# Block 3 of a three-block layer: where the filling of the last state chain and of the attention is emitted, and the order of two small products

## The chip, the core and the metric

The kernel runs on one core of a Trainium2 chip. TensorE (PE) multiplies matrices into PSUM, VectorE (DVE) and ScalarE (ACT) read PSUM and do the elementwise work, GpSimd (POOL) does elementwise work in SBUF, and SP, ACT and POOL issue DMAs. Each engine takes its instructions in one fixed order, and semaphores order the engines among each other. The metric is the device time of one execution in microseconds (us). The median of the three runs before is 3429.2 us (3425.64 to 3435.23).

## What is computed

Three transformer-like blocks run after each other on 512 tokens of width 1024. The change lies in the middle of the third, where a state recurrence (RWKV-7) and a sparse attention (NSA) run side by side and are joined by one output projection:

```python
for l in range(DEPTH):
    h = rmsnorm_3(x, norm1_g[l])
    proj = h @ w_in[l]
    ...
    k_cmp = rmsnorm_3(compress(kv_heads(kc), cmp_pos[l, 0], ...), k_norm_g[l, 0])
    ...
    o_nsa = nsa_attention(q, k_cmp, v_cmp, k_sel, kv_heads(vsl), k_win, kv_heads(vwn), gates, rel_bias)
    ...
    o_rwkv = rwkv7_time_mix(rw, ...)
    x = x + jnp.concatenate([o_nsa, o_rwkv], axis=-1) @ w_out[l]
    # then a convolved feed-forward block

def _wkv7_step(state, inp):
    r, w, k, v, a, b = inp
    sa = jnp.einsum('bhvk,bhk->bhv', state, a)
    state = state * w[:, :, None, :] + sa[..., None] * b[:, :, None, :] + v[..., None] * k[:, :, None, :]
    return state, jnp.einsum('bhvk,bhk->bhv', state, r)
```

## The kernel before

All activations lie features by tokens: a tile is 128 features by 512 tokens. A projection (`K.block`, lines L250 to L252) is 24 matmuls 128x128 by 128x512: eight chunks of the contraction, and three products for each, because both operands are split in a high and a low half (`zh`, `zl`, `wh`, `wl`). Its weights come by one DMA on SP (L239) and are split by ACT (L240) and DVE (L244). Products of the normed input show as `mm<-zh` or `mm<-zl`, those of the output projection as `mm<-nh` or `mm<-nl`. There are two PSUM buffers for such products in this part, two for small products (`s`), two for transposes (`t`) and two for accumulations (`o`).

**The recurrence** (`rwkv`) does two heads at a time, so four head pairs t = 0 to 3, and cuts the 512 tokens in 8 chunks of 64. For each pair `features` makes the operands, `prepare` solves the inside of the chunks, and `steps` walks the 8 chunks, each of which needs the state that the one before it leaves. That is the state chain. One step c is, in the program's order: `rr` (L1809, weight tile 128x64), an ACT copy to `rsb` (L1811), the product that closes the output of the step before (`own`, L1831, weight tiles 64x64), `y` (L1816, 128x64), `sa` (L1819, 64x64), two DVE copies (L1824), the state's product `ds` (L1834, 128x64), a DVE add and a DVE multiply (L1835, L1837). The last gives the next step its state. `finish` then norms the pair's output with two products with a constant (L1630, L483) and gates it (L1853).

**The filling.** A step of the chain leaves TensorE mostly waiting, so other work is emitted between its steps by pulling on Python generators. For t = 0 to 2 that is the preparation of the next pairs. For t = 3 it is `Nsa.prepare`, which makes the attention's keys and values: two weight loads of the compression (L1391, one buffer of 1 MB on SP), its sums on DVE into the one buffer `blk` (L1401), 32 products (L1406), a small chain behind them (L1420, L1426, L1439), and then twice the norm of a key (L483, L488, L489, three DVE operations L460 to L462, L1454, four ACT copies L305 and L307, two DVE operations L306) and the transposes of a value (L1462). Key and value share the one buffer `x3`, into which DVE writes each projection (L1901).

**The attention** (`Nsa.attend`) goes through 16 units: 4 pairs of heads, 2 heads, 2 branches. A unit makes its scores (L1535, L1536), a softmax on DVE, ACT and POOL (L1537, L1543, L1547), transposes (L1555), splits them (L282, L287) and multiplies with the values (L1560, L1561). Before every second unit a generator `prep` projects and norms the next queries (ending at L1492) and makes their compressed scores (L1503). Its filling (`fill`) is the half of the output projection that needs only the recurrence: 8 tiles, each of 12 products `mm<-nh`.

A scheduler fixes the order on each engine from this program text. What is emitted earlier has the right of way, and the slots of a pool with several buffers are given out in the order of emission: a tile emitted later waits for those emitted before it.

```python
for c, _ in enumerate(steps(yo, now)):
    if c < 6 or t == 3:
        next(nxt, None)
    next(more, None)
for _ in more:
    pass
finish(t, yo, bo)
```

Of the kernel before, what the change touches and what calls it, by code (L numbers as in the profile page):

```python
# [1353 lines left out]
class Nsa:  # L1354
# [113 lines left out]
    def attend(self, out, fill):  # L1468

        K, D, proj = self.K, self.D, self.proj  # L1470
        nc, tp = K.nc, K.tp
# [78 lines left out]
        def values(br, g, pt, o, last):  # L1550
            for jj in range(4):
                t = K.st()
                N = 512 - 128 * jj
                for i in range(jj, 4):
                    nc.tensor.transpose(t[:, 128 * (i - jj):128 * (i - jj) + 128],  # L1555
                                        pt[i][:, 128 * (i - jj):128 * (i - jj) + 128], K.ident)
                ph, pl = T("ph", dt=F32R, bufs=3)[:, :N], T("pl", dt=F32R, bufs=3)[:, :N]
                K.split(ph, pl, t[:, :N])
                w = vd[br, g][:, 3 - jj].rearrange("p e d -> p (e d)")
                nc.tensor.matmul(o[:, 512 - N:], w, ph, start=False, stop=False)  # L1560
                nc.tensor.matmul(o[:, 512 - N:], w, pl, start=False, stop=last and jj == 3)  # L1561
# [8 lines left out]
        for k, (j, s, br) in enumerate(units):  # L1570
            if (s, br) == (0, 0):
                nxt = prep(j + 1, ops[j + 1]) if j < 3 else iter(())
            next(nxt, None)
            if (s, br) == (1, 1):
                for _ in nxt:
                    pass
            now = pt
            if k < 15:
                pt = run(*units[k + 1])
            if br == 0:  # L1580
                o = K.so()
                w = vcd[j // 2][s].rearrange("p e d -> p (e d)")
                nc.tensor.matmul(o, w, ops[j][3], start=True, stop=False)
            values(br, j // 2, now, o, br == 1)
            if br == 1:
                K.unstack(out[j][64 * s:64 * s + 64], o)
            if k % 2:
                next(fill, None)
        for _ in fill:
            pass  # L1590
        self.pools.close()
# [2 lines left out]
def rwkv(K, D, proj, out, after):  # L1594

    tc, nc, tp = K.tc, K.nc, K.tp
    V = D["vec"]
    front = ExitStack()
    with K.tc.tile_pool(name="rwb", bufs=1, reuse_waits="tile", side="right") as rp:
# [199 lines left out]
        def steps(yo, sets):  # L1799

            nc.vector.memset(sets[0][3][:64, :, 0], 0.0)
            late = []
            for c in range(8):
                u, n = c // 4, c % 4
                lrb, xt, ml, vs, bk, wend = sets[u]
                w = K.so()
                rr, sa, ds = w[:, :64], w[:, 64:128], w[:64, 128:256]
                for s in range(2):
                    nc.tensor.matmul(rr[64 * s:64 * s + 64], ml[:, s, n, :64], vs[:, s, n], start=True, stop=True)  # L1809
                rs_ = TB("rsb", (P, 64), bufs=2)  # L1810
                nc.scalar.activation(rs_, rr, AF.Copy)  # L1811
                if late:
                    late.pop()()
                y = yo[:, c]
                for s in range(2):
                    nc.tensor.matmul(y[64 * s:64 * s + 64], vs[:, s, n], ml[:, s, n, 64:], start=True, stop=False)  # L1816
                for s in range(2):
                    h = slice(64 * s, 64 * s + 64)
                    nc.tensor.matmul(sa[h], xt[h, n], rs_[h], start=True, stop=True)  # L1819
                if c < 7:  # L1820
                    s0 = TB("s0", (64, 2, 64), bufs=2)
                    nc.vector.tensor_copy(s0, vs[:64, :, n])
                for s in range(2):
                    nc.vector.tensor_copy(vs[:64, s, n], sa[64 * s:64 * s + 64])  # L1824
                ss = TB("ssb", (P, 64), bufs=2)
                nc.scalar.activation(ss[64:], vs[:64, 1, n], AF.Copy)

                def own(y=y, ss=ss, lrb=lrb, vs=vs, n=n):
                    for s, x in enumerate((vs[:64, 0, n], ss[64:])):
                        h = slice(64 * s, 64 * s + 64)  # L1830
                        nc.tensor.matmul(y[h], x, lrb[h, n], start=False, stop=True)  # L1831
                if c < 7:
                    for s in range(2):
                        nc.tensor.matmul(ds[:, 64 * s:64 * s + 64], bk[:, s, n], vs[:, s, n], start=True, stop=True)  # L1834
                    nc.vector.tensor_add(s0, ds.rearrange("p (s d) -> p s d", s=2), s0)  # L1835
                    to = vs[:64, :, n + 1] if n < 3 else sets[1][3][:64, :, 0]
                    nc.vector.tensor_mul(to, s0, wend[:, :, n:n + 1].to_broadcast([64, 2, 64]))  # L1837
                late.append(own)
                if c == 7:
                    late.pop()()  # L1840
                yield

        def finish(t, yo, bo):

            y = K.tp.tile([P, 512], F32, name="tb")
            nc.scalar.activation(y, yo.rearrange("p n l -> p (n l)"), AF.Copy)
            s_ = mean64(y)
            nc.vector.tensor_sub(y, y, s_)
            rg = K.head_rstd(y, R0, 64e-5, rp)
            nc.vector.scalar_tensor_tensor(y, y, V("ln_x_w", t), rg, op0=ALU.mult, op1=ALU.mult)  # L1850
            nc.vector.scalar_tensor_tensor(y, y, V("ln_x_b", t), bo, op0=ALU.add, op1=ALU.add)
            s_ = K.ss()
            nc.tensor.matmul(s_, g2[:, 128 * t:128 * t + 128], xg, start=True, stop=True)  # L1853
            nc.vector.tensor_mul(y, s_, y)
            K.split(*out[t], y)
# [15 lines left out]
        for t in range(4):  # L1871
            bo, now, sets = fs[t][5], sets, []
            more = iter(())
            if t < 3:
                nxt = prepare(t + 1, *fs[t + 1], sets)
                if t < 2:
                    more = fg[t + 2]
            else:
                front.close()
                nxt = after()  # L1880
            yo = K.so([P, 8, 64])
            for c, _ in enumerate(steps(yo, now)):
                if c < 6 or t == 3:
                    next(nxt, None)
                next(more, None)
            for _ in more:
                pass
            finish(t, yo, bo)
# [15 lines left out]
def block3(K, D, hs, store):  # L1904
# [20 lines left out]
    o2 = [[op.tile([P, 512], F32R, name=f"n{e}{n}") for e in "hl"] for n in range(4, 8)]  # L1925
    att = Nsa(K, D, proj)
    rwkv(K, D, proj, o2, att.prepare)
    op = work.enter_context(tc.tile_pool(name="mx3a", bufs=1, reuse_waits="tile", side="right"))
    o1 = [op.tile([P, 512], F32, name=f"o{n}") for n in range(4)]
# [85 lines left out]
```

## Time and profile before

| | |
|---|---|
| median of three runs | 3429.2 us |
| the profiled execution | 3428.05 us |
| its span, first to last instruction | 3426.2 us |
| TensorE busy | 3309.6 us, 97% |
| mean granted TensorE clock | 0.988 of full speed |
| last state chain, first `rr` to last `own` | 2825.7 to 2879.5 us of the span |
| attention, first L1503 to last L1561 | 2902.6 to 3029.5 us |

Times inside the span are counted from its start. "Busy" TensorE means that some matmul is in flight, not that the array is full. A timeline row gives start, duration, engine, line, result and operands; several instructions of a line that follow each other are merged in a row, and an fp32 product shows as two passes, so two products are x4. A duration in brackets is idle time before the row, with what ended it.

### The profile page before, as it was taken

To read this page: it belongs to the slowest core of one execution; us is meant where nothing else is said; L and a number is where in the kernel's file an instruction comes from. 1 tells how busy PE (TensorE), PEld (TensorE's weight loads), DVE (VectorE), ACT (ScalarE), POOL (GpSimd) and SP (SyncE) were. 2 spreads that over 40 slices of the span, in tenths; PEclk is the share of its full clock that TensorE was granted. 3 is DMA by queue.
4 is the path that set the end of the run, shared out by engine and by line. 5 is a ranking of instruction groups with operands and counts; after the bars stand their busy time and mean duration, and the time that the engine had idled before them with its cause. 6 is when DMAs were issued, how large, how long until landed. Compare 5 with 4: busy or idle time off the path is not lost. (4 is left out here: it accounts for less than half of the span.)

```text
span 3426.2 us, 48101 instructions
## 1 busy us (share of the span) xinstructions
PE 3309.6 (97%) x19089; PEld 2717.3 (79%) x19089; DVE 1932.8 (56%) x3242; ACT 1404.0 (41%) x2474; POOL 712.4 (21%) x748
## 2 busy tenths in 40 slices
PE   8999999999999999999999999999999998999999
PEld 8999977778877888876777778788876766778887
DVE  4433366655754433268777564566446656766642
ACT  3222366653433322235555233444333434754431
POOL 2110133332122111112121231111113222421100
PEclk9999999999999999999999999999999999999999
DMA  3223222232223232323332322223331012122332
GB/s 120 90 93 88 86 85 78 69 97 95 66 86 102 92 99 90 96 94 85 106 100 86 111 81 98 92 93 98 104 115 34 31 46 87 41 64 96 98 101 91
DMA packets 89601, 298.61 MB, mean 87 GB/s; under 512 B 10711, under 2 KB 11351, under 8 KB 89120
## 3 DMA queue, kind: packets, MB, share of 16 engines
q1 hardware_dynamic: 76896, 260.70, 23.7%
q0 software_dynamic: 6416, 23.80, 2.4%
q10 hardware_dynamic: 6064, 11.03, 1.0%
q8 instruction: 150, 2.46, 0.3%
q14 instruction: 75, 0.61, 0.1%
HBM read 288.02 MB, written 7.47 MB: 86 GB/s over the span
## 5 line engine op out<-in xcount | busy, mean ns | idle before, releaser
L250 PE MATMUL mm<-zh,wh 128*128 128x512 f32 (+1 forms) x3296 | 1189.8, 361 | 20.2 <-ACT zh L291 8.4
L252 PE MATMUL mm<-zh,wl 128*128 128x512 f32 (+1 forms) x3296 | 1189.0, 361 | 3.8 <-DVE wl L244 3.7
L251 PE MATMUL mm<-zl,wh 128*128 128x512 f32 (+1 forms) x3296 | 1180.2, 358 | 3.1 <-DVE zl L292 3.1
L240 ACT ACTIVATE wh<-w 128x1024 fp32r<-128x1024 f32 (+2 forms) x523 | 523.8, 1001 | 1086.6 <-PE mm L251 759.0
L244 DVE TENSOR_TENSOR wl<-w,wh 128x1024 fp32r<-128x1024 f32 (+2 forms) x523 | 627.6, 1201 | 400.1 <-ACT wh L240 392.3
L250 PEld LDWEIGHTS mm<-zh,wh 128*128 128x128 f32 x3296 | 622.8, 189 | 115.6 <-issue 10.6
L251 PEld LDWEIGHTS mm<-zl,wh 128*128 128x128 f32 x3296 | 623.6, 189 | 100.6 <-DVE zl L292 4.1
L252 PEld LDWEIGHTS mm<-zh,wl 128*128 128x128 f32 x3296 | 622.6, 189 | 100.2 <-DVE wl L244 6.9
L250 PE MATMUL mm<-hh,wh 128*128 128x512 f32 (+1 forms) x880 | 308.5, 351 | 0.0
L251 PE MATMUL mm<-hl,wh 128*128 128x512 f32 (+1 forms) x880 | 308.3, 350 | 0.0
L252 PE MATMUL mm<-hh,wl 128*128 128x512 f32 (+1 forms) x880 | 307.6, 350 | 0.0
L251 PEld LDWEIGHTS mm<-hl,wh 128*128 128x128 f32 x880 | 165.6, 188 | 23.3
L250 PEld LDWEIGHTS mm<-hh,wh 128*128 128x128 f32 x880 | 165.5, 188 | 23.3
L252 PEld LDWEIGHTS mm<-hh,wl 128*128 128x128 f32 x880 | 165.6, 188 | 23.1
L382 POOL TENSOR_TENSOR ta<-ta,rs 128x264 f32<-128x264 f32 (+1 forms) x66 | 86.0, 1316 | 395.8 <-ACT ta L381 395.8
L334 POOL TENSOR_TENSOR acc<-acc,ta 128x512 f32<-128x512 f32 (+1 forms) x49 | 85.2, 1739 | 345.7 <-ACT ta L333 345.3
L1000 POOL TENSOR_TENSOR cv<-cv 128x512 f32<-128x512 f32 x44 | 57.6, 1309 | 434.0 <-DVE cv L981 397.6
L981 DVE SCALAR_TENSOR_TENSOR cv<-ta,vec,cv 128x510 f32<-128x510 f32 (+1 forms) x176 | 132.0, 753 | 3.2 <-ACT cv L978 0.3
L384 DVE TENSOR_TENSOR tb<-mm,ta 128x264 f32<-128x264 f32 (+1 forms) x66 | 32.8, 519 | 141.5 <-PE mm L252 137.7
L380 DVE TENSOR_TENSOR ta<-mm,rs 128x264 f32<-128x264 f32 (+1 forms) x66 | 32.5, 518 | 108.3 <-PE mm L252 108.3
L995 DVE TENSOR_TENSOR ta<-mm,rs 128x512 f32<-128x512 f32 x88 | 60.3, 687 | 57.9 <-PE mm L252 57.8
L282 ACT ACTIVATE hh<-cv 128x512 fp32r<-128x512 f32 x44 | 27.8, 632 | 144.7 <-POOL cv L1000 144.7
(592 smaller groups left out, 4645.3 us busy)
## 6 DMA issues: line engine op xcount, KB each, us to landing
w<-in_w_up_dram SPq DMA_DIRECT2D x176, 512.0 KB, 3.5
w<-in_w_in_dram SPq DMA_DIRECT2D x160, 512.0 KB, 3.5
w<-in_w_dn_dram SPq DMA_DIRECT2D x64, 512.0 KB, 3.5
w<-in_w_dn_dram SPq DMA_DIRECT2D x32, 384.0 KB, 3.1
w<-in_w_out_dram SPq DMA_DIRECT2D x16, 512.0 KB, 3.5
aB<-acum_d POOLq DMA_DIRECT2D x16, 512.0 KB, 5.9
w<-in_w_pb_dram SPq DMA_DIRECT2D x32, 256.0 KB, 2.9
negc<-negc_d POOLq DMA_DIRECT2D x8, 528.0 KB, 4.1
```

Of the source, the lines that this page charges most:

```text
L240: nc.scalar.activation(h_, w_, AF.Copy)
L244: nc.vector.tensor_sub(l_, w_, h_.bitcast(F32))
L250: nc.tensor.matmul(ps, wh, xh, start=start, stop=False)
L251: nc.tensor.matmul(ps, wh, xl, start=False, stop=False)
L252: nc.tensor.matmul(ps, wl, xh, start=False, stop=stop)
L334: nc.gpsimd.tensor_tensor(acc, acc, q, op=ALU.add)
L380: nc.vector.tensor_mul(ta, a, rs[:, c])
L382: nc.gpsimd.tensor_tensor(ta, ta, rs[:, c], op=ALU.mult)
L384: nc.vector.tensor_mul(tb, b, ta)
L981: nc.vector.scalar_tensor_tensor(y[:, d:], x[:, :T - d], w(i), y[:, d:], op0=ALU.mult, op1=ALU.add)
L995: nc.vector.tensor_mul(x, p, rs)
L1000: nc.gpsimd.tensor_tensor(y[1], y[1], y[0], op=ALU.mult)
```

## The change

Three edits. The attention no longer pulls on `fill` after every second unit, so that all of the filling is emitted behind the whole attention. In a step of the chain `sa` is emitted ahead of `y`. And the chain of t = 3 no longer pulls on `nxt`, so that `Nsa.prepare` is emitted behind the whole chain and its `finish`.

```diff
@@ Nsa.attend
             if br == 1:
                 K.unstack(out[j][64 * s:64 * s + 64], o)
-            if k % 2:
-                next(fill, None)
         for _ in fill:
             pass
@@ rwkv, steps
                 if late:
                     late.pop()()
+                for s in range(2):
+                    h = slice(64 * s, 64 * s + 64)
+                    nc.tensor.matmul(sa[h], xt[h, n], rs_[h], start=True, stop=True)
                 y = yo[:, c]
                 for s in range(2):
                     nc.tensor.matmul(y[64 * s:64 * s + 64], vs[:, s, n], ml[:, s, n, 64:], start=True, stop=False)
-                for s in range(2):
-                    h = slice(64 * s, 64 * s + 64)
-                    nc.tensor.matmul(sa[h], xt[h, n], rs_[h], start=True, stop=True)
@@ rwkv, the loop over the pairs
             for c, _ in enumerate(steps(yo, now)):
-                if c < 6 or t == 3:
+                if c < 6 and t < 3:
                     next(nxt, None)
```

No instruction is added or removed; what moves is their order. Lines behind the first edit are two lower in the changed kernel, and `sa` and `y` change places: `rr` is L1807, `sa` L1814, `y` L1817, `own` L1829, `ds` L1832, and in `finish` L1630 is L1628 and L1853 is L1851.

On TensorE, from the end of step 2 to the end of step 3 of the last chain, before:

```order
L1406 MATMUL s<-blk,w_24636 128x62 x16
L1809 MATMUL o<-h_24015,ml 64x64 x2
L1831 MATMUL o<-lrb,ssb 64x64
L1816 MATMUL o<-ml,h_24015 64x64 x2
L1420 MATMUL s<-h_24634,w_24527 64x62
L1819 MATMUL o<-rsb,xt 64x64 x2
L1831 MATMUL o<-lrb,h_24015 64x64
L1426 MATMUL s<-sq,cst 64x62
L1834 MATMUL o<-h_24015,h_24016 64x64 x2
L1439 MATMUL s<-w_24527,h_24731 31x64 x2
L1831 MATMUL o<-lrb,ssb 64x64
L483 MATMUL s<-hsq,cst 128x512
```

The same place in the changed kernel, from the end of step 2 to the first product of step 4:

```order
L252 MATMUL mm<-zh_21368,wl 128x512
L1832 MATMUL o<-h_24015,h_24016 64x64 x2
L1829 MATMUL o<-lrb,ssb 64x64
L1807 MATMUL o<-h_24015,ml 64x64 x2
L1817 MATMUL o<-ml,h_24015 64x64 x2
L1814 MATMUL o<-rsb,xt 64x64 x2
L1829 MATMUL o<-lrb,h_24015 64x64
L1832 MATMUL o<-h_24015,h_24016 64x64 x2
L1829 MATMUL o<-lrb,ssb 64x64
L1807 MATMUL o<-h_24138,ml 64x64 x2
```

The compression's products and the small chain behind them have gone from between the steps. The last filling in the changed chain is the L252 of this piece; the steps 3 to 7 follow each other with nothing between. `y` still stands ahead of `sa` here; over the 32 steps of the four chains it does so 31 times before and 25 times in the changed kernel.

On DVE, in step 2 of the last chain, between the two operations that make the next step's state (L1835 and L1837), before:

```order
L244 TENSOR_TENSOR wl<-w_25150,wh 128x1024
L1835 TENSOR_TENSOR s_24704<-o,s_24704 64x128
L1837 TENSOR_TENSOR h_24015<-s_24704,wend 64x2x64
L1822 COPY s_24784<-h_24015 64x128
L1422 TENSOR_SCALAR kc<-s,vec 64x62
```

The same place in the changed kernel, where the two are L1833 and L1835:

```order
L1833 TENSOR_TENSOR s_24532<-o,s_24532 64x128
L244 TENSOR_TENSOR wl<-w_25150,wh 128x1024
L287 TENSOR_TENSOR nl_21490<-tb,nh_21489 128x512
L1835 TENSOR_TENSOR h_24015<-s_24532,wend 64x2x64
L1820 COPY s_24553<-h_24015 64x128
```

A weight split and the low half of the pair's output have moved in between the two. In the steps 3 to 6 of the changed chain DVE holds nothing but the chain's own operations.

Then, on TensorE, from the end of the chain on in the changed kernel:

```order
L1829 MATMUL o<-lrb,ssb 64x64
L1628 MATMUL s<-tb,cst 128x512
L483 MATMUL s<-hsq,cst 128x512
L1851 MATMUL s<-xg,g_21507 128x512
L1406 MATMUL s<-blk,w_24704 128x62 x16
L1406 MATMUL s<-blk,w_24780 128x62 x16
L1420 MATMUL s<-h_24778,w_24692 64x62
L1426 MATMUL s<-sq,cst 64x62
L1439 MATMUL s<-w_24692,h_24854 31x64 x2
L483 MATMUL s<-hsq,cst 128x512
L1462 MATMUL t<-cst,x_24988 128x128 x4
L250 MATMUL mm<-zh_21302,wh 128x512
```

All of the preparation's small products now stand in one row behind the chain, with no projection between them; the first projection product comes behind the first L1462. Counted over the two orders, the last chain holds 57 projection products and the 32 of L1406 before, and 39 and none in the changed kernel. From the first L1503 to the last L1561 there are 119 products of projections before and 140 in the changed kernel; the last unit that has one between its products is the eleventh before and the twelfth now. Changes of the weight tile's shape from the first chain's start to the first L1503 are 349 before and 342 now.

## Rows read from the trace of the kernel before

**Rows 1.** The page, busy time of an engine, share, instructions.

```profile
PE 3309.6 (97%) x19089; PEld 2717.3 (79%) x19089; DVE 1932.8 (56%) x3242; ACT 1404.0 (41%) x2474; POOL 712.4 (21%) x748
```

**Rows 2.** Stretches of chain and attention: length, busy per engine, PEclk, DMA share, GB/s.

```profile
2855.50:2860.50 5.00, 1.76 (x21) 1.19 (x20) 4.01 (x20) 3.38 (x11) 0.00 (x0) 1.00 0.26 61
2860.50:2874.50 14.00, 10.31 (x53) 7.06 (x53) 9.37 (x20) 6.68 (x14) 6.08 (x5) 0.51 0.12 36
2874.50:2902.50 28.00, 27.02 (x119) 19.31 (x118) 18.30 (x32) 15.08 (x26) 7.56 (x8) 1.00 0.34 121
2902.50:3001.00 98.50, 90.63 (x491) 70.77 (x491) 80.15 (x266) 66.88 (x185) 39.00 (x64) 0.98 0.12 42
3001.00:3030.60 29.60, 23.05 (x108) 16.19 (x106) 17.74 (x58) 18.17 (x55) 8.21 (x16) 0.88 0.07 19
```

**Rows 3.** TensorE's waits from 2902 to 3030.5: total, times, longest.

```profile
PE s L1503 <- DVE x L1492: 3.9, 4, 1.2
```

**Rows 4.** Timeline of TensorE, step 3 of the last chain and step 4's start.

```profile
2851.34 0.34 PE L1809 MATMUL o<-h,ml 128*64 128x64 f32 x4
...
2852.23 0.33 PE L1819 MATMUL o<-rsb,xt 64*64 64x64 f32 x4
...
2860.55 0.48 PE L1809 MATMUL o<-h,ml 128*64 128x64 f32 x4 [0.53 <-DVE h L1837]
```

**Rows 5.** Timeline of ACT and DVE, the same step's own operations.

```profile
2851.78 0.22 ACT L1811 ACTIVATE rsb<-o 128x64 f32<-128x64 f32 x1
...
2852.66 0.47 DVE L1824 COPY h<-o 64x64 f32<-64x64 f32 x2
...
2853.79 0.28 DVE L1835 TENSOR_TENSOR s<-o,s 64x128 f32<-64x128 f32 x1 [0.65 <-PE o L1834]
...
2854.33 0.27 DVE L1837 TENSOR_TENSOR h<-s,wend 64x128 f32<-64x128 f32 x1
```

**Rows 6.** Timeline, a weight split on DVE and the finish's first operation on ACT.

```profile
2834.85 1.22 DVE L244 TENSOR_TENSOR wl<-w,wh 128x1024 fp32r<-128x1024 f32 x1 [2.33 <-PE mm L252]
...
2879.54 0.60 ACT L1846 ACTIVATE tb<-o 128x512 f32<-128x512 f32 x1 [1.11 <-PE o L1831]
```

**Rows 7.** Timeline, operations of the key's norm on DVE and ACT.

```profile
2861.06 0.68 DVE L461 SCALAR_TENSOR_TENSOR hsq<-hsq,hrs 128x512 f32<-128x512 f32 x1
...
2866.39 0.63 ACT L307 ACTIVATE kh<-x 64x512 fp32r<-64x512 f32 x1
...
2867.36 0.69 DVE L1901 TENSOR_TENSOR x<-mm,rs 128x512 f32<-128x512 f32 x1
...
2879.50 0.75 DVE L1454 SCALAR_TENSOR_TENSOR x<-x,vec,hrs 128x512 f32<-128x512 f32 x1
```

**Rows 8.** Timeline, the issue on SP of the compression's second weight load.

```profile
2841.80 0.33 SPq L1391 DMA_DIRECT2D w<-in_cmp_w_dram  x1
```

**Rows 9.** DMA issues from 2800 to 2900, KB each, median us to landing.

```profile
w<-in_cmp_w_dram SPq DMA_DIRECT2D x2, 1024.0 KB, 4.8
```

**Rows 10.** Timeline, from the compression's last product to the first value transposes.

```profile
2853.68 0.41 PE L1439 MATMUL s<-w,h 128*31 128x64 f32 x4
...
2868.11 1.12 PE L1462 MATMUL t<-cst,x 128*128 128x128 f32 x4 [0.45 <-DVE x L1901]
```

**Rows 11.** Timeline of TensorE, projection products at the lower clock.

```profile
2870.78 0.63 PE L251 MATMUL mm<-zl,wh 128*128 128x512 f32 x1
2871.20 0.63 PE L252 MATMUL mm<-zh,wl 128*128 128x512 f32 x1
```

**Rows 12.** The same at full clock, behind products of a smaller weight tile.

```profile
2823.39 0.50 PE L252 MATMUL mm<-zh,wl 128*128 128x512 f32 x1
2823.73 0.39 PE L250 MATMUL mm<-zh,wh 128*128 128x512 f32 x1
2823.96 0.40 PE L251 MATMUL mm<-zl,wh 128*128 128x512 f32 x1
```

**Rows 13.** Timeline of TensorE, the second group of the compression's products.

```profile
2847.62 3.78 PE L1406 MATMUL s<-blk,w 128*128 128x62 f32 x32
```

## The prediction

> **What bounds the kernel now.** The page comes first: TensorE is busy for 3309.6 of 3426.2 us, DVE for 56% and the others for less [rows 1]. Nothing is added to TensorE or taken from it here, so the time can change only through TensorE's waits, its clock, and small costs between products. The windows over the part that is reordered come next [rows 2]: between 2855.5 and 2902.5, the second half of the last state chain and what follows up to the attention, TensorE is not busy for 3.24 + 3.69 + 0.98 = 7.9 us, and in the attention for 7.87 + 6.55 = 14.4 us. For 14 us of the chain the granted clock is 0.51, the lower of the two levels (1.2 GHz). It fell after the stretch in which TensorE was busy for 1.76 of 5 us. Behind 3036 the feed-forward block runs on the full engine, so what this part wins or loses goes whole into the time. In the attention the waits are spread over many small ones; a kind that comes back is the wait for the next queries, 3.9 in four times [rows 3].
>
> Then I read one step of the chain, engine by engine. Step 3 issues `rr` at 2851.34 and `sa` at 2852.23 [rows 4]; between them stands the ACT copy of 0.22 [rows 5]. The DVE copies start 0.43 behind `sa` and take 0.47, L1835 starts 0.66 after them, with `ds` between [rows 5]; L1837 could follow after 0.32 (it stood behind one small foreign operation), and takes 0.27. With 0.15 more to the next `rr` the round trip is 3.2 us, of which TensorE works at most the 1.76 of [rows 2]. Step 4 took 5.0 us from `rr` to `rr`: 2855.5 to 2860.55 [rows 2, 4]; its extra came from foreign work on ACT and DVE.
>
> **The change part by part.** The sum is made against the profiled execution's 3428.05 us, which is 1.2 below the median of three. I count what TensorE waits or loses in the part, after less before.
>
> *The chain loses its cover.* Before, the chain and the preparation of the attention's keys, both chains of small dependent operations, ran inside each other. In the new order the chain's first three steps keep projection products (39 instead of 57), and the steps 3 to 7 have nothing. At the end of step 2, DVE does a weight split of 1.22 [rows 6] and an operation of 0.69 (the size of L1901 [rows 7]) between L1835 and L1837: 1.9 us, and `rr` is queued behind that. I take 2.0 (bounds 0, if the weights come late enough to be done earlier in another gap, and 2.0). A bare step costs between 3.2, the round trip, and 5.0, the step with foreign work. On DVE the new steps hold only the chain's operations, so I take 3.6: 3.6 - 1.76 = 1.84 of waiting in each of four steps, 7.4 us, and 1.5 in the last, which has no `ds`. That is 8.9 us (bounds 7 and 15).
>
> *The finish is bare.* L1630 waits for an ACT copy of 0.60 and its start, 0.9 in all; L483 waits for a DVE operation of 0.69 and an ACT operation of 0.63 with the gaps between, 1.6 [rows 6, 7]. Together 2.5 (bounds 1.5 and 3.5). Before, projection products covered both.
>
> *The second weights of the compression.* SP issues this load only when the first group of L1406 has released the one buffer: at 2841.80 [rows 8]. It lands in 4.8 us [rows 9]. Projection products covered that; now the second L1406 stands directly behind the first on TensorE, and everything behind it waits too: 4.8 us (bounds 3 and 5.8). The sums on DVE for the second group run in the same gap.
>
> *The small chain and the key's norm.* Three round trips through another engine (L1420 to L1426, to L483, and the later L483 behind the second L1901) cost about the 0.9 that `rr` to `sa` costs, 2.7 (bounds 1.5 and 3.5). Then L1462 has to wait for the whole norm of the first key, since the value's projection goes into the same buffer `x3`: six ACT operations of 0.63, three DVE operations of 0.68, one of 0.75 and one of 0.69, that is 7.3 us [rows 7], and about 2 for the copies of the compressed values that stand ahead of them on ACT and DVE. I take 9.4. The bounds are 6, if part of it runs beside L483, and 12.9, the 14.4 us from L1439 to L1462 before [rows 10] less the 1.5 of TensorE's own work between. No product of the filling stands between L483 and L1462 now. Then 2.0 before the attention's first products, where the queries' norm waits with 1.2 [rows 3] and fewer products before it.
>
> *The clock.* At the lower level a projection product comes every 0.42 us [rows 11] instead of every 0.23 [rows 12]. Before, the low stretch held 10.31 us of busy time at that rate [rows 2], a loss of some 4. Now TensorE is less than half busy from step 3 to L1462, and about 22 us of work at full speed lie there (five steps at up to 1.76, the finish, L1406 with twice 3.78 [rows 13], the key's products, and the first projections after it). I take a loss of 10 (bounds 4 and 22).
>
> A rule of the Trainium skill bears on that. The page "TensorE: Matmul & The Clock Gate", Part 1, says that the array's clock is gated by how busy the engine has been, and that an idle engine falls to half rate. The trace agrees with a granted 0.51 behind the bare step. By the rule without any recovery in between, all 22 us would be lost, and the sum below would end 12 higher.
>
> *The attention gains something.* 21 projection products more lie in it (140 for 119), so there is more to fill with, and the products reach one unit further. The last four units stay bare, as the last five were. Of the 14.4 us without work and some 3 of lower clock (0.98 and 0.88 granted [rows 2]) I take 4 back (bounds: 3 worse, and 17, all of it). The units' own path through DVE, ACT and POOL is as long as before, and most of TensorE's small waits there are for it; this is why I take a value near the small end.
>
> *The grouping.* Between two shapes of weight tile a product starts late: L250 starts 0.34 behind the L252 that follows a 64-row tile, and the next one 0.23 later [rows 12], so a change costs 0.11. The new order has 342 changes for 349: 0.7 us less. The page "TensorEngine Tiling (Array Packing)" of the Trainium skill, Key Properties, says that a change of tiling mode drains the engine, which speaks for the edit. By it, two drains fewer in each of 31 steps would be 62 x 0.11 = 6.8 us, and the sum 3447; but the order shows `y` still ahead of `sa` in 25 of 32 steps, since `y` is ready while `rsb` is not.
>
> *The sum.* After: 2.0 + 8.9 + 2.5 + 4.8 + 2.7 + 9.4 + 2.0 + 10 = 42.3. Before: 7.9 + 4 = 11.9. The chain's part grows by 30.4, the attention gives back 4, the shapes 0.7: + 25.7. 3428.05 + 25.7 = 3453.8; I say **3453 us**.
>
> **The rivals.**
> (a) *The attention pays it back.* With filling free to go wherever a unit waits, the 128 us from the first L1503 to the last L1561 could lose all their waits and their low clock: 17 instead of 4 back, 3453 - 13 = 3440. For it speaks that units 10 and 11 get 20 products where they had 2; against it that the last four units stay bare, and that 6.55 of the 14.4 lie there and just before. It decides if the stage, with 4.9 us (21 x 0.23) more work, ends in 116 us. Then the result is on the edge of no change, 0.3% (10 us) being about what a measurement of this kernel can tell from none.
> (b) *Alone, the small operations run faster than beside others.* From step 2 to the first L1462 ACT and DVE carry hardly anything but the dependent operations themselves, so each stretch takes the sum of its own durations, TensorE idles less and the clock falls no longer than before: 1.2 at step 2, 7 for the bare steps (3.2 each), 1.5 for the finish, 4.8 for the load, 1.5 for the trips, 6 for the norm, 1 for the queries, a loss of 4; together 27.0, less 11.9 and 4.7: + 10.4, 3438. That is not slower by the measure above. For it speaks how clean DVE's new order is in steps 3 to 6; against it the 5.0 of step 4, and that POOL's work on the filling still runs there. It decides if the way from the last `own` to the first L1462 is under 28 us.
> (c) *The clock stays down and the norm is as long as it was.* + 12 and + 3.5 over the forecast: 3468. For it speaks the 0.51 that 5 us of a bare step brought.
>
> **How the numbers follow.** Forecast 0.63, (a) 0.10, (b) 0.10, (c) 0.14, and 0.03 for what is not seen here, (a) and (b) together above all (3425). The likeliest alone lies between 3440 and 3464. The range reaches from (b) to (c): 3437 to 3468. Slower by over 0.3% (above 3439.5): the forecast, (c) and a little of (a), 0.79. Within 0.3%: (b) and most of (a), 0.17. Faster: 0.04.
>
> **What would show it.** In the changed profile: steps 3 to 6 of the last chain at 3.2 to 4 us each with no projection product between them; a wait of some 5 us of L1406 for a DMA on its weights; a wait of 7 to 11 us of L1462 for DVE; a granted clock near 0.5 over some 25 to 40 us where it was 14; the first L1503 some 20 to 26 us later than 2902.6 counted from the chain's start, and the attention within 5 us of its 128. The prediction is wrong if the way from the chain's first `rr` to the first L1503 grows by less than 10 us, or if the attention shortens by more than 10.

## The result and the profile after

| | before | after |
|---|---|---|
| median of five runs | 3428.89 us (3425.64 to 3435.23) | 3450.38 us (3447.92 to 3465.41) |
| ratio, 95% interval | | 1.0072 [1.0058, 1.0085] |

The change makes the kernel slower, by 21 us between the medians and by 25 us as the ratio has it. The profiled execution of the changed kernel is the one of 3465.41 us, 15 us above the median of its runs; it spent more time at the lower clock than the others (0.978 granted, the others 0.983 to 0.985), so its rows overstate that part.

TensorE's busy time on the page answers to [rows 1]: TensorE is busy for 24 us more with the same work, since products take longer at the lower clock, and the clock line shows where (before, all 40 of its digits are 9).

```profile
PE 3333.3 (96%) x19089; PEld 2732.4 (79%) x19089; DVE 1935.7 (56%) x3242; ACT 1405.9 (41%) x2474; POOL 709.3 (20%) x748
...
PEclk9999999999999999999999999999999986989999
```

The next view cuts the profiled execution at two places that both kernels have: from the last chain's first `rr` to the attention's first L1503, and from there to the last L1561. The windows of the kernel before:

```profile
2825.70:2902.60 76.90, 68.09 (x393) 48.33 (x391) 49.63 (x126) 34.50 (x73) 18.93 (x18) 0.91 0.27 89
2902.60:3029.50 126.90, 113.68 (x597) 86.96 (x597) 97.35 (x321) 83.89 (x235) 47.21 (x80) 0.96 0.11 37
```

And of the changed kernel (columns as in [rows 2]: length, busy time of PE, PEld, DVE, ACT, POOL, granted clock, DMA):

```profile
2835.40:2938.70 103.30, 77.33 (x372) 53.70 (x371) 48.15 (x122) 34.58 (x71) 16.90 (x18) 0.70 0.19 64
2938.70:3064.80 126.10, 118.33 (x618) 91.12 (x618) 100.12 (x325) 85.71 (x237) 46.57 (x80) 0.95 0.11 39
```

The first stretch grew by 26.4 us, although 19 projection products (4.4 us at the 0.23 of [rows 12]) have left it. So 30.8 us more are lost in it: TensorE's time without work went from 8.8 (76.90 - 68.09) to 26.0 (103.30 - 77.33), which is 17.2; the other 13.6 are work at the lower clock (0.70 granted for 0.91) and late starts. The attention got 0.8 us shorter with 21 products (4.8 us) more in it, so it lost 5.6 less than before. The rest of the span's 37.5 us is not this change's doing or not plainly: 5.7 lie ahead of the first chain, where both orders are the same, 4.1 in the first three chains, and 2.2 behind the attention.

Where TensorE waited from step 2 to the attention, by line and releaser (total, times, longest):

```profile
PE t L1462 <- DVE x L1899: 8.6, 2, 8.2
PE s L1406 <- DMA w<-in_cmp_w_dram: 5.5, 1, 5.5
PE o L1807 <- DVE h L1835: 3.7, 5, 1.4
PE o L1829 <- DVE h L1822: 1.9, 5, 0.4
PE s L483 <- ACT hsq L495: 1.4, 1, 1.4
PE o L1829 <- ACT ssb L1824: 0.9, 1, 0.9
PE s L1628 <- ACT tb L1844: 0.7, 1, 0.7
PE s L1426 <- ACT sq L1424: 0.7, 1, 0.7
```

And the same as a row in time, on TensorE's timeline; a bracket is the wait ahead of the row:

```profile
2856.37 0.34 PE L1807 MATMUL o<-h,ml 128*64 128x64 f32 x4 [1.19 <-DVE h L1835]
...
2859.78 0.48 PE L1807 MATMUL o<-h,ml 128*64 128x64 f32 x4 [0.38 <-DVE h L1835]
...
2864.30 0.48 PE L1807 MATMUL o<-h,ml 128*64 128x64 f32 x4 [1.38 <-DVE h L1835]
...
2867.82 0.48 PE L1807 MATMUL o<-h,ml 128*64 128x64 f32 x4 [0.38 <-DVE h L1835]
...
2871.40 0.48 PE L1807 MATMUL o<-h,ml 128*64 128x64 f32 x4 [0.38 <-DVE h L1835]
...
2874.86 2.08 PE L1628 MATMUL s<-tb,cst 128*128 128x512 f32 x2 [0.69 <-ACT tb L1844]
2878.38 2.07 PE L483 MATMUL s<-hsq,cst 128*128 128x512 f32 x2 [1.44 <-ACT hsq L495]
...
2882.62 7.09 PE L1406 MATMUL s<-blk,w 128*128 128x62 f32 x32 [0.46 <-DVE hsq L460]
2895.21 7.06 PE L1406 MATMUL s<-blk,w 128*128 128x62 f32 x32 [5.51 <-DMA w<-in_cmp_w_dram]
...
2904.74 2.08 PE L483 MATMUL s<-hsq,cst 128*128 128x512 f32 x2 [0.37 <-DVE vc L1441]
2915.06 1.12 PE L1462 MATMUL t<-cst,x 128*128 128x128 f32 x4 [8.24 <-DVE x L1899]
...
2938.74 0.43 PE L1503 MATMUL s<-kcd,x 128*128 128x64 f32 x2 [0.98 <-DVE x L1492]
```

Read it beside [rows 10, 13]: the same L1406 took 3.78 between the steps of the chain and takes 7.09 here, at the lower clock, with nothing to follow it. The wait for the second weights begins when the first L1406 ends, since there is one buffer, as [rows 8] showed.

### The profile page after: what moved, and what is told of

It reads as the page before. It is cut to its first block, busy times and chain, and to the rows that moved or that the text cites. A ratio compares the mean times of both kernels' runs of the same rounds, so it can differ in the third digit from the quotient of the medians.

```text
span 3463.7 us, 48108 instructions
## 1 busy us (share of the span) xinstructions
PE 3333.3 (96%) x19089; PEld 2732.4 (79%) x19089; DVE 1935.7 (56%) x3242; ACT 1405.9 (41%) x2474; POOL 709.3 (20%) x748
## 5 line engine op out<-in xcount | busy, mean ns | idle before, releaser
L252 PE MATMUL mm<-zh,wl 128*128 128x512 f32 (+1 forms) x3296 | 1189.7, 361 | 3.3 <-DVE wl L244 3.2
L252 PEld LDWEIGHTS mm<-zh,wl 128*128 128x128 f32 x3296 | 623.0, 189 | 97.7 <-DVE wl L244 6.6
L252 PE MATMUL mm<-hh,wl 128*128 128x512 f32 (+1 forms) x880 | 307.6, 350 | 0.0
L252 PEld LDWEIGHTS mm<-hh,wl 128*128 128x128 f32 x880 | 165.6, 188 | 23.3
```

The costliest lines, as they stand in the source:

```text
L252: nc.tensor.matmul(ps, wl, xh, start=False, stop=stop)
```

## The experiments

The theories: (1) the whole loss is the third edit's, by two chains of dependent operations that now run after each other; (2) the attention's new filling costs too; (3) the lower clock makes most of the loss, not the waits. Ratios are to the kernel before on the same chip, in five rounds, with their 95% intervals; 0.001 is 3.4 us.

**One edit at a time.** The third edit alone:

```diff
-                if c < 6 or t == 3:
+                if c < 6 and t < 3:
                     next(nxt, None)
```

> The kernel before with the third edit alone: the chain of t = 3 doesn't pull on the keys' preparation. Theory 1 (the whole loss comes from this edit: two chains of small dependent operations that ran inside each other now run one after the other): +20 to +26 us over the kernel before, about 3449 to 3455, and the way from the last chain's first rr to the first L1503 as long as in the changed kernel, 100 to 105 us. Theory 2 (the attention's new filling costs as well): under +15. Theory 3 (the waits are there, but the lower clock makes most of the loss): no other time than theory 1 here.

Measured: 1.0058 [1.0046, 1.0071], + 20 us; 3448.16. Its first stretch takes 98.2 us, a little under the 100 to 105 expected, and the waits in it are the same ones. The second row is its attention, 124.9 us for 126.9 with the 21 products (4.8 us) that left the first stretch: so it gives back 6.8 without the first edit.

```profile
2826.80:2925.00 98.20, 74.12 (x371) 50.37 (x369) 47.88 (x122) 33.38 (x71) 16.23 (x18) 0.74 0.19 65
2925.00:3049.90 124.90, 116.15 (x618) 89.78 (x618) 100.49 (x325) 85.75 (x237) 46.83 (x80) 0.97 0.13 41
```

```profile
PE t L1462 <- DVE x L1901: 8.2, 1, 8.2
PE s L1406 <- DMA w<-in_cmp_w_dram: 4.9, 1, 4.9
```

The first edit alone:

```diff
-            if k % 2:
-                next(fill, None)
         for _ in fill:
             pass
```

> The first edit alone: the half output projection is emitted behind the whole attention. Theory 1: between -4 and +3 us against the kernel before. Theory 2: +5 or more. If the attention alone gains by having its filling free, -4 or better.

Measured: 0.9991 [0.9982, 0.9999], a gain of 3 us with an interval that nearly touches none. The attention is the place: 121.9 us for 126.9, of which 0.7 are three products that went elsewhere, and the clock stays up.

```profile
2900.50:3022.40 121.90, 111.14 (x594) 82.95 (x594) 98.59 (x323) 83.94 (x235) 46.68 (x80) 1.00 0.12 38
```

The second edit alone (`sa` ahead of `y`, the middle piece of the change's diff):

```diff
+                    nc.tensor.matmul(sa[h], xt[h, n], rs_[h], start=True, stop=True)
                 y = yo[:, c]
...
-                    nc.tensor.matmul(sa[h], xt[h, n], rs_[h], start=True, stop=True)
```

> The second edit alone: sa emitted ahead of y. All theories: between -1 and +1 us against the kernel before, since y is ready while sa's operand is not, and y stays ahead in most steps. If every change of the weight tile's shape drained TensorE for 0.11 us twice in a step, -6.8.

Measured: 1.0018 [1.0008, 1.0027], 6 us slower. All theories missed this. In its trace the stretch from the last chain's first `rr` to L1503 is 80.3 us for 76.9, with two products more. The cut at step 2 shows the difference: `own` waits 0.79 for DVE (0.31 before), and behind it the second group of L1406 runs into the lower clock, 5.67 us for the 3.78 of [rows 13]. Before:

```profile
2846.99 0.33 PE L1831 MATMUL o<-lrb,h 64*64 64x64 f32 x2 [0.31 <-DVE h L1824]
```

With the second edit alone:

```profile
2852.14 0.32 PE L1831 MATMUL o<-lrb,h 64*64 64x64 f32 x2 [0.79 <-DVE h L1824]
2852.39 0.45 PE L1834 MATMUL o<-h,h 128*64 128x64 f32 x4
2852.77 5.67 PE L1406 MATMUL s<-blk,w 128*128 128x62 f32 x32
```

```profile
2846.84:2852.77 5.93, 5.14 (x35) 3.55 (x34) 5.62 (x23) 2.44 (x5) 0.00 (x0) 1.00 0.51 177
2852.77:2858.37 5.60, 5.60 (x35) 5.48 (x33) 1.49 (x4) 0.00 (x0) 0.00 (x0) 0.64 0.14 47
2858.37:2864.90 6.53, 6.16 (x33) 3.56 (x32) 3.11 (x15) 3.23 (x13) 0.00 (x0) 0.50 0.00 1
```

In the kernel before, the granted clock is still 1.00 there and falls only at the end of step 4 [rows 2]. Why it falls here is not shown: TensorE was busy for 5.14 of 5.93 us ahead of L1406 and for all of 5.60 us while L1406 ran. A test of where the 6 us arise is the last run of this section.

The first two edits without the third:

```diff
-            if k % 2:
-                next(fill, None)
...
+                    nc.tensor.matmul(sa[h], xt[h, n], rs_[h], start=True, stop=True)
                 y = yo[:, c]
```

> The first and the second edit without the third. Theory 1: between -5 and +3 us against the kernel before, so that the third edit alone stands between this kernel and the changed one, with 20 to 25 us. Theory 2: +5 or more.

Measured: 1.0002 [0.9993, 1.0010]. So + 20 (third), - 3 (first) and + 6 (second) make 23, and the whole change measured + 25. Theory 2 is out: the attention's filling pays a little.

**What in the third edit costs.** The preparation is emitted behind the chain, and also behind `finish`. Only the second is undone here:

```diff
+            if t == 3:
+                for _ in nxt:
+                    pass
             finish(t, yo, bo)
-        for _ in nxt:
-            pass
```

> The changed kernel with one statement moved: for t = 3 the rest of the keys' preparation is emitted ahead of finish instead of behind it. Theory 1, with the slots as the cause (the pool of small products gives its slots out in the order of emission, so that the preparation's first product L1406 can't start before the three products of finish have theirs): L1406, L1420, L1426, L1439 and the first L483 come back between the steps of the chain, though the preparation is still emitted behind the whole chain, and most of the loss goes, -10 to -22 us against the changed kernel. If it is the place of the emission itself (lower right of way than the chain), the loss stays: within 4 us of the changed kernel.

Measured: 0.9992 [0.9984, 1.0001], 3425.5 us, 27 us less than the changed kernel by the ratios, where 10 to 22 less was expected. The whole loss is gone, with all three edits still in place but for this statement. The order of the preparation against the chain was never the cost: its products came back between the steps, and `finish` stands behind them, between projections.

```profile
2846.78 1.28 PE L1406 MATMUL s<-blk,w 128*128 128x62 f32 x10
...
2847.99 0.34 PE L1807 MATMUL o<-h,ml 128*64 128x64 f32 x4
...
2857.19 2.89 PE L1406 MATMUL s<-blk,w 128*128 128x62 f32 x24
...
2860.01 0.34 PE L1807 MATMUL o<-h,ml 128*64 128x64 f32 x4
...
2888.30 1.02 PE L1628 MATMUL s<-tb,cst 128*128 128x512 f32 x2
```

What held L1406 back in the changed kernel was the slot: L1406 needs one of the two `s` buffers, and the three `s` tiles of `finish`, emitted earlier, had the first claim, though they could not be filled before the chain's end. The changed kernel's rows show it: the sums for the first L1406 are done at 2836, and L1406 starts at 2882.62, when DVE's L460 has read the product of `finish`'s L483 out of its buffer:

```profile
2834.65 1.40 DVE L1401 TENSOR_TENSOR blk<-xa,pos 128x62 f32<-128x62 f32 x8
...
2881.87 0.69 DVE L460 SCALAR_TENSOR_TENSOR hsq<-s,hrs 128x512 f32<-128x512 f32 x1 [4.21 <-ACT hrs L489]
```

A third `s` buffer, with the order left alone, would have been the direct test; it was not run.

**The one buffer that key and value share.** The changed kernel with two buffers for `x3`:

```diff
-                x = cp.tile([P, 512], F32, name="x3")
+                x = cp.tile([P, 512], F32, name="x3", bufs=2)
```

(both places of it)

> The changed kernel with two buffers for x3, so that a value's projection doesn't wait for the norm of the key. Its order has 59 projection products in steps 2 to 6 of the last chain, which were bare; behind the chain the finish and the compression's products stand bare as before, and the value's L1462 that now stands behind the norm is the second one. Theory 1: the steps' waits (7 to 9 us) go and a part of the 8.2 us of L1462 stays, -8 to -15 us against the changed kernel. Theory 3 (clock): -15 or more, since TensorE stays busy through the chain. If one buffer didn't matter: within 3 us.

Measured: 1.0038 [1.0025, 1.0051], 12 us faster than the changed kernel's 1.0072. In its profiled execution, at 3456 the slowest of five and 15 above their median, the steps 3 to 6 are full of projections, the 8.2 at L1462 shrinks to 1.5, and what is left behind the chain is the rest of theory 1: the load, and the key's norm at another instruction, L483.

```profile
PE s L483 <- ACT hsq L495: 6.2, 2, 4.6
PE s L1406 <- DMA w<-in_cmp_w_dram: 5.0, 1, 5.0
PE t L1462 <- DVE x L1899: 1.5, 1, 1.5
```

The same edit on the first two edits without the third:

```diff
 (the first two edits, as above)
-                x = cp.tile([P, 512], F32, name="x3")
+                x = cp.tile([P, 512], F32, name="x3", bufs=2)
```

> The first two edits without the third, with two buffers for x3. If the bare steps of the kernel before (7.9 us of waits and some 4 of lower clock from 2855 to 2902) come from the one buffer that key and value share: -5 to -10 us against the kernel before. If something else holds the projections back: within 3 us of it.

Measured: 0.9995 [0.9985, 1.0005], no difference that can be told, where 5 to 10 us less was expected.

And on the kernel before, by itself:

```diff
-                x = cp.tile([P, 512], F32, name="x3")
+                x = cp.tile([P, 512], F32, name="x3", bufs=2)
```

> The kernel before with two buffers for x3 and nothing else. The same as for the run above, without the two edits: -5 to -10 us against the kernel before if the one buffer made its chain bare, within 3 us otherwise.

Measured: 0.9977 [0.9968, 0.9986], 3420.89 us, 8 us faster than the kernel before. The steps 4 to 6 were mostly bare because the value's projection had to wait for the key's norm; now TensorE is busy through them at the full clock, where it was busy for 17.07 of 24 us at a granted 0.72 from 2855.5 to 2879.5:

```profile
2856.60:2879.60 23.00, 22.55 (x137) 14.52 (x136) 19.47 (x46) 15.32 (x33) 6.10 (x6) 1.00 0.19 53
```

Beside the first two edits, in the run above, most of this gain is gone.

**The clock.** The changed kernel with 21 products that nobody reads, put where TensorE waits (this adds work):

```diff
+                if pad and c > 2:
+                    nc.tensor.matmul(w[:64, 256:], rs_, K.all[:, :256], start=True, stop=True)
...
+                if i == 0:
+                    e = K.st()
+                    for _ in range(5):
+                        nc.tensor.matmul(e[:62], h, K.all, start=True, stop=True)
...
+                if br == 0:
+                    e = K.st()
+                    for _ in range(7):
+                        nc.tensor.matmul(e[:62], kc, K.all[:64], start=True, stop=True)
```

(and one behind `ds`, like the first)

> The changed kernel with 21 added products whose results nobody reads, in the places where TensorE waits: in each of the steps 3 to 7 one behind sa and (but for the last) one behind ds, 64x256, five of 62x512 behind the first group of L1406, and seven of 62x512 ahead of the L1462 that waits. The order of all else is kept. They add work, some 16 us of products that lie in waits. If the lower clock, which follows on TensorE's waiting, is a good part of the loss (theory 3, and the term of 10 us in my forecast): -5 to -12 us against the changed kernel, and a granted clock near 1 from 2856 on. If the waits alone make the loss and the clock costs nothing: 0 to +4 us.

Measured: 1.0081 [1.0068, 1.0095], 3 us above the changed kernel's ratio and within both intervals. It doesn't decide: the products did not bring the clock back, so what a full clock would have been worth here was not tested by it. Nor did they stay inside the waits: from `rr` to `rr` the steps 3 to 6 take 4.4 to 6.0 us, where they took 3.4 to 4.5. From step 4 to the end of the chain TensorE was busy for 15.43 of 20.38 us at a granted 0.50, and later for 26.10 of 28.30 at 0.64:

```profile
2846.35:2866.73 20.38, 15.43 (x82) 7.63 (x82) 4.50 (x16) 3.83 (x10) 3.75 (x3) 0.50 0.12 39
2866.73:2879.36 12.63, 9.24 (x39) 5.32 (x39) 3.77 (x6) 3.58 (x6) 1.27 (x1) 0.72 0.09 23
2879.36:2907.66 28.30, 26.10 (x74) 11.47 (x75) 13.12 (x44) 7.65 (x20) 1.24 (x2) 0.64 0.11 37
```

**Versions that might beat both.** The first edit with two buffers for `x3`:

```diff
-            if k % 2:
-                next(fill, None)
...
+                x = cp.tile([P, 512], F32, name="x3", bufs=2)
```

> The kernel before with the first edit and two buffers for x3. The buffer alone gave -8 us, the first edit alone -2.5. If they add up: -9 to -13 us against the kernel before; if the filling that the buffer pulls into the chain is what the attention would have used: -5 to -8.

Measured: 0.9983 [0.9974, 0.9992], 3420.68 us: no better than the buffer alone, so the two gains do not add. From here to the run with both edits and the buffer (0.9995) there is only the second edit: 4 us more, with the sign that it had alone, but the two intervals overlap.

The first and the third edit, the third mended as above, with two buffers and without the second edit:

```diff
-            if k % 2:
-                next(fill, None)
...
-                if c < 6 or t == 3:
+                if c < 6 and t < 3:
...
+            if t == 3:
+                for _ in nxt:
+                    pass
             finish(t, yo, bo)
...
+                x = cp.tile([P, 512], F32, name="x3", bufs=2)
```

> The kernel before with the first edit, with the keys' preparation of t = 3 emitted behind the chain but ahead of finish (the third edit, mended), with two buffers for x3, and without the second edit. If the third edit, mended, is worth what it was beside the other two (about -3 us): -9 to -14 us against the kernel before. If finish, now late, delays the attention's filling: -3 to +3.

Measured: 0.9985 [0.9976, 0.9994], 3423.09 us, 5 us less and between the two cases expected. Below the kernel before, but not below the buffer alone, which is the best that was found.

**The second edit, where it costs.** `sa` ahead of `y` in the chains t = 0 to 2 alone:

```diff
+                for f in ((do_sa, do_y) if first else (do_y, do_sa)):
+                    f()
...
-            for c, _ in enumerate(steps(yo, now)):
+            for c, _ in enumerate(steps(yo, now, t < 3)):
```

> The kernel before with sa ahead of y in the chains of t = 0 to 2 alone. The second edit in all four chains made the kernel 6 us slower (ratio 1.0018), against my expectation of nothing. If that comes from the last chain, where the trace shows a longer wait in step 2 and the lower clock 6 us earlier: -1 to +2 us here. If it comes from the covered chains: +3 to +7.

Measured: 1.0010 [1.0001, 1.0019], 3.4 us, at the low end of the second case, with an interval that reaches into the first. So the first three chains probably have a part in the 6 us; how large it is stays open. The one profiled execution of this kernel was its fastest and shows no place.

## Why the prediction came out as it did

The time was forecast as 3453 and is 3450.4, and the cause is the one that it named: the edit alone that puts the preparation behind chain and `finish` costs 20 us, and undoing its place against `finish` takes all of it back. The prediction took the bare order as given and added up what it costs; that the place behind `finish` makes it bare, and not the one behind the chain, it did not say. By its own steps, in the profiled execution:

- *The end of step 2*, forecast 2.0: 0.89 ahead of `own` and 1.19 ahead of `rr`, 2.1. On DVE a weight split of 1.21 and an L287 of 0.68 stand between L1833 and L1835, as the order let expect.
- *The bare steps*, forecast 3.6 each and 8.9 of waiting: from `rr` to `rr` 3.41, 4.52, 3.52 and 3.58, so the length was right but for the 4.52, which the last section explains. The waiting in them is 5.0 only (L1807 3.7 - 1.2, L1829 1.9, L1814 0.6). At the lower clock TensorE works for 2.7 to 2.8 us of a step of 3.5, where 1.76 was taken, and waits for 0.75 to 0.9, where 1.84 was taken. The sum counted some 4 us twice, once as a wait and once in the clock's term.
- *The finish*, forecast 2.5: 0.69 + 1.44 = 2.1, and 0.46 more ahead of L1406.
- *The second weights*, forecast 4.8: 5.51.
- *The three round trips*, forecast 2.7: 0.66 ahead of L1426, 0.37 ahead of L483, and nothing ahead of the later L483, which has four projection products in front of it: 1.0. The second L1462 waits for another 0.32.
- *L1462 behind the key's norm*, forecast 9.4: 8.24, with the copies of the compressed values ahead of the norm on ACT and DVE as said.
- *The queries*, forecast 2.0: 0.98.
- *The clock*, forecast a loss of 10 for 4 before. What the stretch lost beside its waits grew by 13.6 in this execution, which had the clock low for longer than the others: 0.50 in the windows from 2860 to 2903, and 0.79 to 2940. The 25 to 40 us that were given for it are too short for this execution, and for the third edit alone too, whose profiled execution is within 1 us of its median: 0.74 granted over 98.2 us is some 51 us at the lower level. Over 195 runs of the kernel before, the changed one and the eleven experiments without added work, with a constant for each kernel, a mean clock lower by 0.001 goes with 1.8 us (standard error 0.1). By that the 0.0059 between the means of the two kernels (0.9828 and 0.9887) go with 11 of the 25 us between their mean times. That is a relation, not an experiment; the run that was to test it didn't raise the clock. So theory 3, as "most of the loss", is not borne out, and "a good part of it" is likely and not shown.
- *The attention*, forecast 4 back: 5.6 in the trace. It comes with the 21 products, as forecast: the third edit alone, which moves them, gives back 6.8. The first edit alone gains 3 us [0.3, 6.2] with three products fewer in the attention.
- *The grouping*, forecast 0.7 back: this step failed. The edit costs 6.2 us [2.7, 9.2] by itself. The price per change of shape was not the point; two products that change places alter what the scheduler puts where, and in step 2 of the last chain the wait became longer and the clock fell two steps earlier. That is one place; the first three chains seem to have a part, and the cause of the whole 6 us stays open. Its mean clock is lower by 0.0023, which goes with 4 of the 6 us by the relation above. The trace of this edit alone has 337 changes of shape from the first chain to the first L1503, for 338 in the trace of the kernel before, so it doesn't test what a change costs. The rule on drains of the page "TensorEngine Tiling (Array Packing)" of the Trainium skill, Key Properties, from which the prediction made 6.8 us less by two drains fewer in each of 31 steps, is neither borne out nor refuted by these runs.

The waits were forecast to grow by 24.4 (32.3 less 7.9) and grew by 17.2, so 7 too much; the rest, the clock above all, by 6, and it grew by 13.6, so 8 too little. About 4 of these are one error seen from two sides, the bare steps' time put down as waiting. The stretch as a whole was forecast to lose 30.4 more and lost 30.8, but that agreement is partly luck, since 30.8 is from the slowest execution. With the third edit alone the stretch loses 26.1 (98.2 - 76.9, and 4.8 for 21 products less), so the 30.4 were some 4 too many for this edit; its attention gives back 6.8 of the 26.1, which leaves the 20 of its time. In the time of the whole change the second edit, forecast at nothing, makes up for the 4. The largest difference between the two traces is the first L1406, 3.78 us there, at the full clock, and 7.09 here.

Of the rivals: (a) needed 17 back in the attention, which gave 5.6. (b) needed less than 28 us from the last `own` to the first L1462; it was 41.4 (2873.71 to 2915.06). (c) is what the profiled execution looks like, 3465; the median is not there.

## What to carry to other kernels

Where slots of a pool are given out in the order of emission, ask of a piece that is emitted later not only what it must follow by its data but whose slots it now waits for: here one statement's place against `finish` was worth some 27 us (1.0072 to 0.9992), and the same preparation emitted behind the whole chain, but ahead of `finish`, cost nothing. A stretch without filling is priced as the sum of its engines' round trips; don't add a clock's loss on top of waits that the same slower engine makes shorter. And look for the buffer that keeps filling out of the waits before the order is changed: a second buffer of 2 KB per partition for `x3` was worth 8 us.

## What was not expected of the hardware

In the second bare step of the changed kernel, DVE's L1835 took 1.28 us and the copy behind it (L1820) 1.18, where they take 0.28 and 0.22 in the other steps, while POOL ran two sums of 1.27 each in SBUF:

```profile
2862.74 2.54 POOL L1941 TENSOR_TENSOR h<-h,acc 128x512 f32<-128x512 f32 x2 [20.41 <-ACT h L1940]
2862.88 1.28 DVE L1835 TENSOR_TENSOR h<-s,wend 64x128 f32<-64x128 f32 x1
2864.19 1.18 DVE L1820 COPY s<-h 64x128 f32<-64x128 f32 x1
```

That is the step of 4.52. It came again with the third edit alone (1.27 and 1.17 beside L1943), and in the kernel before DVE's L1454 took 1.50 us beside the same sums, for the 0.75 of [rows 7]. The page "SBUF — State Buffer" of the Trainium skill, section "SBUF: two separate sides", says that DVE and GpSimd share a pair of ports, which one of them holds for a whole instruction while the other is blocked; the rows agree, each DVE operation ending about when a POOL sum does.

Then, that TensorE can be busy at the lower clock for long: with the added products 15.43 of 20.38 us at a granted 0.50 and 26.10 of 28.30 at 0.64, and with the second edit alone 5.60 of 5.60 at 0.64. "Busy" here means that some product is in flight.
